# First loads of a two-layer decoder trunk: weight pieces of two contraction blocks, the first weight rounded by VectorE, and narrower zero products ahead of them

## The chip, the core and the metric

The kernel runs on one core of one Trainium2 chip. The metric is the device time of one execution in microseconds (us), as the median of several runs. A profile is taken of one execution; its span is the time from the first to the last instruction that the profile shows, and the execution's own time is a little longer than that span. Engines are named as in the profile: PE is TensorE's matmul, PEld its weight load, DVE is VectorE, ACT is ScalarE, POOL is GpSimd, and SP (SPq) is SyncE, which here only issues DMAs.

## The reference, cut to what matters

The program computes two decoder layers on 1024 tokens of 1024 features, in float32. The first has a causal Conformer convolution, the second has windowed attention; each is followed by a layer norm, an MLP with a squared ReLU, a second norm, and a gated embedding. Only the beginning bears on this change:

```python
def conformer_conv(x, w_in, b_in, w_dw, b_dw, ln_g, ln_b, w_out, b_out):
    h = x @ w_in + b_in                       # (1024 x 1024) @ (1024 x 2048)
    a, gate = jnp.split(h, 2, axis=-1)
    h = a * jax.nn.sigmoid(gate)
    ...                                       # depthwise conv, norm, silu, w_out

def reference(x, p, ...):
    for i in range(DEPTH):
        y = conformer_conv(x, ...) if i < N_A_LAYERS else swa_sink_attention(...)
        x = layer_norm(DEEPNORM_ALPHA * x + y, mix_ln_g[i], mix_ln_b[i])
        x = layer_norm(DEEPNORM_ALPHA * x + sq_relu_mlp(x, ...), mlp_ln_g[i], mlp_ln_b[i])
        x = x + (p[i] @ ple_w_proj[i]) * jax.nn.sigmoid(x @ ple_w_gate[i])
    return x
```

## The kernel before, in words

**Products in three parts.** Every large product is made of float32 values split in two: a rounded high part (`xh`, `wh`: a cast to the type fp32r) and a low part, the difference of value and high part (`xl`, `wl`). `split` does this with an ACT cast and a DVE subtraction. `mm3` then issues three matmuls for each product: high by high, high by low, low by high.

**The start.** `conv` calls `warm_up` (line 918), which clears a tile `t` of 128x512 on DVE and issues `WARM` = 8 matmuls of it on PE. Their result is used by nothing. Then the first chunk of the input product is loaded. The contraction over 1024 features is cut into eight blocks kb = 0 to 7. For each block come a slice of the transposed input, 128x512 (256 KB, into a tile `X`: 512 of the 1024 tokens), and a piece of the first weights, 128x256 (128 KB, a quarter of a tile `raw` of 128x1024; `raw` of blocks 0 to 3 and `raw` of blocks 4 to 7). `prep` with `blocks` (line 552) does this: for each block it issues two DMAs, the weight piece first except in block 0, and splits the weight piece (ACT cast to `wh`, DVE subtraction to `wl`) and the input slice (ACT cast to `xh`, DVE subtraction to `xl`). `conv_in` then issues, block by block, two products (gate and value, into two PSUM tiles), hence six matmuls of 128x512 for each block, 48 in all. After them the second 512 tokens follow with the same weights.

**What sets the order.** The program is first recorded as a list of operations, and `Recorder.schedule` then places all of them, of the whole program, in one order for each engine: it keeps a time for every engine, gives each operation an estimated duration (`cost`) and takes the operation of least number among those that are ready. A few operations may go to either DVE or POOL. Tiles come from numbered slots, which are handed on when the last user of the earlier tile is placed as done. So a change in the first operations shifts the planner's times for everything later, and with them the order in which operations that are ready at about the same time are placed. The planner counts a 512-column matmul as 227 ns, one of 128 columns as 109 ns, and a DMA's landing by its size and by how many came before it. On the chip the engines run these orders as they are, each in its own queue, and wait on semaphores.

**The rest.** After the first chunk come seven more chunks of input weights, five of them through forms that save one product in eight; the depthwise convolution as small matmuls `ps<-B,E` of 128x256, fed by an exchange through DRAM (`scr`); norms; the MLP, with intermediate values in DRAM (`hid`); attention; the second MLP; and the output.

Of the kernel before, what the change touches and what calls it, by code (L numbers as in the profile page):

```python
# [10 lines left out]
F32 = mybir.dt.float32  # L11
F32R = mybir.dt.float32r
AF = mybir.ActivationFunctionType
ALU = mybir.AluOpType

P = 128
# [4 lines left out]
HT = 512  # L21
# [32 lines left out]
             ps=6, tr=2, sc=0, pv=0, mid=0)  # L54
# [7 lines left out]
FORM_HOMES = ("A", 9), ("bo", 2), ("v", 1), ("B", 4), ("X", 8)  # L62
LATE = 50
SOONER = 200
WARM = 8
LOW_BY = 500
EMBED_BY = (300, 0)
MARK = (1, 2)
# [457 lines left out]
class Emit:  # L526
# [36 lines left out]
    def prep(self, ap, blocks=None, low=None, halves=False):  # L563

        nc = self.nc
        if halves:
            wh = nc.tile("wh", (P, 1024), F32R)
            wl = nc.tile("wl", (P, 1024), F32R)
            for w, src in ((wh, ap), (wl, low)):
                nc.sync.dma_start(w.bitcast(F32)[:, 0 : low.n], src)  # L570
            return wh, wl
        raw = nc.tile("raw", (P, 1024), F32)
        wh = nc.tile("wh", (P, 1024), F32R)
        wl = nc.tile("wl", (P, 1024), F32R)
        if blocks:
            for j, kb in enumerate(blocks):
                cs = slice(j * 256, (j + 1) * 256)
                x = self.sb("X")
                for w, k in ((x, 0), (raw[:, cs], 1))[:: -1 if kb else 1]:
                    nc.sync.dma_start(w, ap[:, cs] if k else self.d["xT"][kb, :, 0:HT])  # L580
                self.split(raw[:, cs], wh[:, cs], wl[:, cs])
                self.split(x, *self.xs(kb, 0, HT))
            return wh, wl
        if low is not None:
            c = slice(0, low.n)
            nc.sync.dma_start(raw[:, c], ap)
            nc.scalar.copy(wh[:, c], raw[:, c])
            nc.sync.dma_start(wl.bitcast(F32)[:, c], low)
            return wh, wl
        nc.sync.dma_start(raw, ap)  # L590
        nc.scalar.copy(wh, raw)
        nc.vector.tensor_tensor(out=wl, in0=raw, in1=wh.bitcast(F32), op=ALU.subtract)
        return wh, wl
# [324 lines left out]
    def warm_up(self):  # L918

        nc = self.nc  # L920
        z = self.sb("t", F32R)
        nc.vector.memset(z.bitcast(F32), 0.0)
        ps = self.ps()
        for k in range(WARM):
            nc.tensor.matmul(ps, z[:, 0:P], z, start=True, stop=True)

    def load_xT(self, h, kb):
        raw = self.sb("X")
# [1448 lines left out]
```

## Time and profile before

| | us |
|---|---|
| median of 3 runs | 2090.38 |
| lowest and highest of them | 2089.67 and 2091.93 |
| the profiled execution's own time | 2089.28 |
| its span in the profile | 2087.6 |
| PE busy in the span | 2077.5 |
| DVE busy | 1688.1 |
| ACT busy | 1228.2 |
| POOL busy | 275.2 |

The profile's page gives the busy time of each engine and a chain of waits that ended last. The timeline lists instructions by start and duration, with the idle time before them and what ended it in square brackets, where it was idle. The view by windows gives the busy time of each engine in stretches of the span, with the number of instructions, the granted clock of TensorE (PEclk), the share of the DMA engines' time that was busy, and the rate moved. A matmul's modelled duration overlaps the next one's, so its pace is read from start to start.

### The profile page before, as it was taken

Reading aid. Unit: us, or ns where it says so; the run is one execution under the profiler, and the core shown is the slowest. Engines: PE = TensorE matmul, PEld = TensorE weight load, DVE = VectorE, ACT = ScalarE, POOL = GpSimd, SP = SyncE. Lnnn points to the kernel's source line nnn. Section 1 sums busy time; section 2 is a strip of 40 time slices with the busy share of each in tenths; the row PEclk is TensorE's granted clock in tenths of the full one; section 3 lists DMA queues with packets and bytes.
Section 4 is the critical chain, followed back from the end, with each engine's and each line's share of the span. In section 5 each row is a group of like instructions: output and inputs, shape, how many; then the busy total and the mean of one; then the engine's idle time right before and its main releaser. Section 6 shows DMA issues by size and latency. Waiting matters only on the chain.

```text
span 2087.6 us, 29481 instructions
## 1 busy us (share of the span) xinstructions
PE 2077.5 (100%) x9784; PEld 1731.2 (83%) x9784; DVE 1688.1 (81%) x2628; ACT 1228.2 (59%) x2268; POOL 275.2 (13%) x512
## 2 busy tenths in 40 slices
PE   9999999999999999999999999999999999999999
PEld 7888888888888888888888888888888888888877
DVE  8999796878876789986983677869788778888688
ACT  6767656856655644454752678866666573333374
POOL 0524111000000000001220366500000000000041
PEclk9999999999999999999999999999999999999999
DMA  6669855988995879876468685698888886575636
GB/s 227 189 205 298 284 196 176 339 288 285 306 307 193 309 274 312 276 265 242 165 220 295 227 289 196 191 338 303 270 296 296 290 298 202 183 246 173 236 112 206
DMA packets 249864, 521.96 MB, mean 250 GB/s; under 512 B 25456, under 2 KB 64112, under 8 KB 249712
## 3 DMA queue, kind: packets, MB, share of 16 engines
q1 hardware_dynamic: 249712, 520.09, 73.8%
q8 instruction: 77, 1.26, 0.2%
q14 instruction: 75, 0.61, 0.1%
HBM read 348.81 MB, written 168.56 MB: 248 GB/s over the span
## 4 chain that ended last, share of the span: by engine, by line
PE 91%; DVE 4%; ACT 2%; DMA 2%; issue 1%; POOL 1%; SPq 0%; DVEq 0%; ACTq 0%; POOLq 0%
PE ps L493 74%; PE tr L493 18%; DVE g L493 1%; ACT z L493 1%; DVE sm L493 1%; POOL sm L493 1%; DVE E L493 0%; DMA raw<-in_w_in_dram 0%; DVE z L493 0%; DMA z<-in_w_dw_dram 0%; DVE t L493 0%; DMA A<-mid 0%; DVE wl L493 0%; DMA raw<-in_w_up_dram 0%; DVE B L493 0%
## 5 line engine op out<-in xcount | busy, mean ns | idle before, releaser
L493 PE MATMUL ps<-xh,xl 128*128 128x512 f32 x618 | 240.4, 389 | 0.0
L493 PE MATMUL ps<-xl,xh 128*128 128x512 f32 x618 | 240.4, 389 | 0.0
L493 PE MATMUL ps<-xh 128*128 128x512 f32 x618 | 240.4, 389 | 0.0
L493 PE MATMUL ps<-xh,wh 128*128 128x512 f32 x588 | 230.5, 393 | 0.4 <-DVE g L493 0.4
L493 PE MATMUL ps<-xl,wh 128*128 128x512 f32 x588 | 230.3, 392 | 0.2 <-DVE xl L493 0.2
L493 PE MATMUL ps<-xh,wl 128*128 128x512 f32 x588 | 230.3, 392 | 0.0
L493 POOL TENSOR_SCALAR sm<-sm 128x1 f32<-128x1 f32 x72 | 26.5, 370 | 1397.4 <-DVE E L493 1209.0
L493 PE MATMUL ps<-wh,xh 128*128 128x512 f32 x436 | 172.3, 397 | 1.6 <-DVE t L493 0.9
L493 PE MATMUL ps<-wl,xh 128*128 128x512 f32 x436 | 172.4, 396 | 0.0
L493 PE MATMUL ps<-wh,xl 128*128 128x512 f32 x436 | 172.2, 396 | 0.0
L493 ACT CAST wh<-raw 128x1024 fp32r<-128x1024 f32 (+2 forms) x134 | 119.6, 894 | 80.7 <-PE ps L493 49.9
L493 DVE TENSOR_TENSOR wl<-raw,wh 128x1024 fp32r<-128x1024 f32 (+2 forms) x100 | 99.3, 995 | 50.7 <-ACT wh L493 50.0
L493 ACT CAST wh<-g 128x512 fp32r<-128x512 f32 x136 | 81.1, 619 | 96.5 <-PE ps L493 40.5
L493 ACT CAST xh<-wh 128x1024 fp32r<-128x1024 f32 x76 | 79.8, 1050 | 96.1 <-PE ps L493 74.9
L493 PEld LDWEIGHTS ps<-xh 128*128 128x128 f32 x618 | 116.0, 188 | 24.2
L493 PEld LDWEIGHTS ps<-xh,xl 128*128 128x128 f32 x618 | 116.0, 188 | 24.1
L493 PEld LDWEIGHTS ps<-xl,xh 128*128 128x128 f32 x618 | 116.0, 188 | 23.9
L493 PEld LDWEIGHTS ps<-xh,wh 128*128 128x128 f32 x588 | 110.8, 188 | 23.1 <-DVE g L493 0.8
L493 PEld LDWEIGHTS ps<-xh,wl 128*128 128x128 f32 x588 | 110.6, 188 | 22.8
L493 PEld LDWEIGHTS ps<-xl,wh 128*128 128x128 f32 x588 | 110.8, 188 | 22.6 <-DVE xl L493 0.5
L493 DVE TENSOR_TENSOR xl<-wh,xh 128x1024 fp32r<-128x1024 f32 x76 | 92.7, 1220 | 25.3 <-ACT xh L493 25.3
L493 ACT ACTIVATE t<-t 128x512 f32<-128x512 f32 x144 | 90.8, 632 | 36.1 <-DVE t L493 34.5
(407 smaller groups left out, 5430.6 us busy)
## 6 DMA issues: line engine op xcount, KB each, us to landing
wh<-hid SPq DMA_DIRECT2D x78, 512.0 KB, 4.7
raw<-in_w_up_dram SPq DMA_DIRECT2D x68, 512.0 KB, 4.3
wl<-in_w_down_dram SPq DMA_DIRECT2D x58, 512.0 KB, 5.4
hid<-zz SPq DMA_DIRECT2D x96, 256.0 KB, 4.8
hid<-t SPq DMA_DIRECT2D x64, 256.0 KB, 5.1
z<-in_w_dw_dram SPq DMA_DIRECT2D x56, 288.0 KB, 4.1
raw<-hid SPq DMA_DIRECT2D x30, 512.0 KB, 4.7
A<-mid SPq DMA_DIRECT2D x48, 256.0 KB, 4.8
```

The source lines that it names most:

```text
L493: getattr(getattr(nc, o.eng), o.name)(*a, **k)
```

## The change

There are four edits, all at the start of the program:

- `WARM` is 14 in place of 8, and the cleared tile is the first 128 columns of `t`, so that each of the zero products has 128 columns in place of 512.
- Weight pieces are loaded by a table `PIECES`: blocks 0 and 1 have a piece of their own (128x256), blocks 2, 4 and 6 fetch a piece for two blocks (128x512, 256 KB), and blocks 3, 5 and 7 fetch none. ACT's cast and DVE's subtraction work on the same pieces.
- The rounding of block 0's weight piece is a DVE copy in place of an ACT cast.
- The order in the record is: in block 0 the input slice and then the weight piece; in all others the weight piece, its split, and then the input slice.

```diff
-WARM = 8
+WARM = 14
+PIECES = 1, 1, 2, 0, 2, 0, 2, 0
...
             for j, kb in enumerate(blocks):
-                cs = slice(j * 256, (j + 1) * 256)
+                n = PIECES[kb]
+                cs = slice(j * 256, (j + n) * 256)
                 x = self.sb("X")
-                for w, k in ((x, 0), (raw[:, cs], 1))[:: -1 if kb else 1]:
-                    nc.sync.dma_start(w, ap[:, cs] if k else self.d["xT"][kb, :, 0:HT])
-                self.split(raw[:, cs], wh[:, cs], wl[:, cs])
+                src = self.d["xT"][kb, :, 0:HT]
+                if kb == 0:
+                    nc.sync.dma_start(x, src)
+                if n:
+                    nc.sync.dma_start(raw[:, cs], ap[:, cs])
+                    (nc.scalar.copy if kb else nc.vector.tensor_copy)(wh[:, cs], raw[:, cs])
+                    nc.vector.tensor_tensor(out=wl[:, cs], in0=raw[:, cs], in1=wh[:, cs].bitcast(F32), op=ALU.subtract)
+                if kb:
+                    nc.sync.dma_start(x, src)
                 self.split(x, *self.xs(kb, 0, HT))
...
-        z = self.sb("t", F32R)
+        z = self.sb("t", F32R)[:, 0:P]
         nc.vector.memset(z.bitcast(F32), 0.0)
         ps = self.ps()
         for k in range(WARM):
-            nc.tensor.matmul(ps, z[:, 0:P], z, start=True, stop=True)
+            nc.tensor.matmul(ps[:, 0:P], z, z, start=True, stop=True)
```

What this makes of the queues is seen in three places. Line 493 before and line 494 after are the same line of the recorder, through which every operation is issued. First the DMA queue of SP, from the program's first DMA on: `X_31` to `X_36` are the input slices of blocks 0 to 5, `raw_1` holds the weights of blocks 0 to 3 and `raw_2` those of blocks 4 to 7. Before:

```order
L493 DMA X_31_95<-in_xT_dram 128x512
L493 DMA raw_1_65<-in_w_in_dram 128x256 x2
L493 DMA X_32_96<-in_xT_dram 128x512
L493 DMA raw_1_65<-in_w_in_dram 128x256
L493 DMA X_33_97<-in_xT_dram 128x512
L493 DMA raw_1_65<-in_w_in_dram 128x256
L493 DMA X_34_98<-in_xT_dram 128x512
L493 DMA raw_2_66<-in_w_in_dram 128x256
L493 DMA X_35_99<-in_xT_dram 128x512
```

And of the change:

```order
L494 DMA X_31_95<-in_xT_dram 128x512
L494 DMA raw_1_65<-in_w_in_dram 128x256 x2
L494 DMA X_32_96<-in_xT_dram 128x512
L494 DMA raw_1_65<-in_w_in_dram 128x512
L494 DMA X_33_97<-in_xT_dram 128x512
L494 DMA X_34_98<-in_xT_dram 128x512
L494 DMA raw_2_66<-in_w_in_dram 128x512
L494 DMA X_35_99<-in_xT_dram 128x512
```

The slice of block 2 (`X_33`) is the sixth DMA in both, but block 3's weights now travel ahead of it; the slice of block 3 (`X_34`) has the same bytes ahead of it in one DMA fewer.

Second the queue of DVE, from its first instruction (the clearing of the tile for the zero products) on, with `xl_242` and `wl_8` as the low parts of blocks 0 to 3. Before:

```order
L493 MEMSET t_53_117 128x512
L493 TENSOR_TENSOR xl_242_306<-X_31_95,xh_241_305 128x512
L493 TENSOR_TENSOR wl_8_72<-raw_1_65,wh_3_67 128x256 x2
L493 TENSOR_TENSOR xl_242_306<-X_32_96,xh_241_305 128x512
L493 TENSOR_TENSOR wl_8_72<-raw_1_65,wh_3_67 128x256
L493 TENSOR_TENSOR xl_242_306<-X_33_97,xh_241_305 128x512
L493 TENSOR_TENSOR wl_8_72<-raw_1_65,wh_3_67 128x256
```

And of the change:

```order
L494 MEMSET t_53_117 128x128
L494 CAST wh_3_67<-raw_1_65 128x256
L494 TENSOR_TENSOR xl_242_306<-X_31_95,xh_241_305 128x512
L494 TENSOR_TENSOR wl_8_72<-raw_1_65,wh_3_67 128x256 x2
L494 TENSOR_TENSOR xl_242_306<-X_32_96,xh_241_305 128x512
L494 TENSOR_TENSOR wl_8_72<-raw_1_65,wh_3_67 128x512
L494 TENSOR_TENSOR xl_242_306<-X_33_97,xh_241_305 128x512
```

The cast of block 0's weights stands ahead of block 0's first subtraction, and the subtraction for blocks 2 and 3 is one instruction, ahead of block 2's `xl`.

Third the queue of PE some 300 rows into the program, in the depthwise convolution (`ps<-B,E`) among a later chunk's products (`ps_400`), with a group of four transposes (`tr_81`). Before:

```order
L493 MATMUL ps_400_879<-xh_245_309,wh_388_823 128x512
L493 MATMUL ps_400_879<-xl_246_310,wh_388_823 128x512
L493 MATMUL ps_400_879<-xh_245_309,wl_389_826 128x512
L493 MATMUL ps_418_1016<-B_413_979,E_41_105 128x256 x2
L493 MATMUL tr_81_145<-ident_303,g_402_911 128x2x4x16 x4
L493 MATMUL ps_418_1016<-B_413_979,E_41_105 128x256 x7
```

And of the change:

```order
L494 MATMUL tr_81_145<-ident_303,g_399_882 128x2x4x16 x4
L494 MATMUL ps_400_887<-xh_245_309,wl_390_824 128x512
L494 MATMUL ps_400_887<-xh_245_309,wh_389_821 128x512
L494 MATMUL ps_400_887<-xl_246_310,wh_389_821 128x512
L494 MATMUL ps_400_887<-xh_245_309,wl_390_824 128x512
L494 MATMUL ps_418_1014<-B_412_976,E_41_105 128x256 x9
```

No edit touches this part of the program: the planner placed the transposes some six matmuls sooner. Such shifts stand in all queues, in the convolution and the first norms above all, and again in attention and near the end. The number of instructions on each engine changes only by the edits: PE issues 6 matmuls more, DVE 2 instructions fewer, ACT 4 fewer, SP 3 fewer, POOL the same.

## The prediction

> **What bounds the kernel now.** I read the page first, then what PE waited for (us in total, times, longest), then two stretches of the view by windows (engine busy times, then PEclk, DMA share, GB/s).
>
> ```profile
> span 2087.6 us, 29481 instructions
> ...
> PE 2077.5 (100%) x9784; PEld 1731.2 (83%) x9784; DVE 1688.1 (81%) x2628; ACT 1228.2 (59%) x2268; POOL 275.2 (13%) x512
> ```
>
> ```profile
> PE ps L493 <- DVE t L493: 2.4, 2, 1.5
> PE tr L493 <- ACT t L493: 1.1, 1, 1.1
> PE ps L493 <- DVE z L493: 0.5, 3, 0.2
> PE ps L493 <- DVE xh L493: 0.5, 1, 0.5
> PE ps L493 <- DVE g L493: 0.4, 1, 0.4
> PE ps L493 <- ACT t L493: 0.3, 1, 0.3
> PE ps L493 <- DVE xl L493: 0.2, 1, 0.2
> ```
>
> ```profile
> 20.00:50.00 30.00, 30.00 (x134) 24.82 (x134) 29.29 (x48) 19.51 (x33) 0.00 (x0) 1.00 0.56 204
> 2000.00:2088.00 88.00, 82.37 (x395) 67.79 (x393) 72.95 (x119) 48.49 (x88) 19.26 (x23) 0.99 0.56 188
> ```
>
> PE is idle for 10.1 us of the span (2087.6 - 2077.5). Most of it is the program's two ends: 1.5 us ahead of the first matmul, and part of the 5.6 in the last stretch (88.00 - 82.37). Its waits on other engines are 5.4 us in all; without the first 1.5 and the 0.2 for `xl`, which are at the start, 3.7 are left for all the rest of the program. So PE bounds nearly everything, and an edit counts by the PE time that it frees or spoils. The profiled execution took 2089.28, 1.10 below the median of 2090.38; that much is added to every sum below. A measurement of this kernel can tell about 0.2% from no change: 4.2 us, so faster means below 2086.2 and slower above 2094.6.
>
> The start is the exception, since there PE runs on what has landed. The timeline of PE, then that of ACT, then the chain of waits:
>
> ```profile
> 1.51 3.78 PE L493 MATMUL ps<-t 128*128 128x512 f32 x8 [1.51 <-DVE t L493]
> 5.09 1.05 PE L493 MATMUL ps<-xh,wh 128*128 128x512 f32 x2
> 5.94 1.03 PE L493 MATMUL ps<-xl,wh 128*128 128x512 f32 x2
> 6.79 0.65 PE L493 MATMUL ps<-xh,wl 128*128 128x512 f32 x2
> ...
> 9.46 0.50 PE L493 MATMUL ps<-xl,wh 128*128 128x512 f32 x1 [0.22 <-DVE xl L493]
> ```
>
> ```profile
> 3.57 0.62 ACT L493 CAST xh<-X 128x512 fp32r<-128x512 f32 x1 [1.50 <-DMA X<-in_xT_dram]
> 4.10 0.40 ACT L493 CAST wh<-raw 128x256 fp32r<-128x256 f32 x1
> ```
>
> ```profile
> 3.12 4.92 DMA X<-in_xT_dram
> ...
> 8.06 0.63 ACT xh L493
> ...
> 9.46 70.00 PE ps L493 x325
> ```
>
> Two things are to be seen. **First**, block 0's operands were ready at 4.50 (4.10 + 0.40), but its first matmul started at 5.09, right behind the eight zero products. **Second**, the chain does not go through that. The start ends at 9.46, when block 2's `xl` exists: its slice was issued at 3.12 and landed at 8.04, and after ACT's cast, which ends at 8.69, DVE's subtraction takes the rest. From 9.46 PE runs 70 us without a gap.
>
> **The change, part by part.**
>
> *Zero products.* Matmuls of 512 columns start 0.427 us apart up to 6.79 (0.85 for each pair: 5.09, 5.94, 6.79) and later
>
> ```profile
> 12.13 0.39 PE L493 MATMUL ps<-xh,wh 128*128 128x512 f32 x1
> 12.36 0.39 PE L493 MATMUL ps<-xl,wh 128*128 128x512 f32 x1
> 79.46 0.44 PE tr L493 x4
> ```
>
> 0.227 apart: half pace until about 7.0. (PEclk is 1.00 in the window 6 to 7 below as well, so here it is the spacing that shows the pace.) The clearing,
>
> ```profile
> 0.97 0.48 DVE L493 MEMSET t<- 128x512 f32 x1 [0.97 <-PEq L2369]
> ```
>
> gets a quarter of the columns: between 0.12 and 0.48 us; PE then starts between 1.15 and 1.51. No row has a 128-column product at half pace. Below, a quarter of 0.427 is 0.107 each, 1.5 us for 14; above, the transposes of 128 columns take 0.11 each at full pace, times 0.427/0.227 is 0.21, 2.9 us. The zeros end between 2.7 and 4.4. I take 4.2, since the transpose row is a matmul of this width.
>
> *First weight on DVE.* DVE has been idle since 1.45. No row shows this copy; the nearest is
>
> ```profile
> 262.59 0.41 DVE L493 CAST xh<-t 128x512 fp32r<-128x512 f32 x1
> ```
>
> twice its columns, so it takes 0.2 to 0.41. ACT's cast of the same piece showed no wait at 4.10, so the piece was there by then: `wh` is ready between 3.8 and 4.5, and `xh` at 4.19. If the copy ends after 4.19 it holds back block 0's `xl` behind it on DVE, by 0.3 at most; that is wanted only two matmuls (0.85) later. So block 0 starts at about 4.3 rather than 5.09, a gain of 0.8 there (0.55 to 0.85).
>
> *Two-block pieces.* They remove three DMAs, three ACT casts and three DVE subtractions of 128x256. None of those was on the chain: ACT took block 2's slice at 8.06, 0.02 after it landed. What counts is the DMA order. Ahead of block 2's slice there were 128 KB of weights for blocks 0, 1 and 2 each; now block 3's go ahead too. The rate in the neighbourhood:
>
> ```profile
> 6.00:7.00 1.00, 1.00 (x4) 0.80 (x3) 0.69 (x1) 0.45 (x2) 0.00 (x0) 1.00 0.62 162
> 8.00:9.00 1.00, 1.00 (x5) 0.53 (x3) 0.29 (x1) 0.93 (x2) 0.00 (x0) 1.00 1.04 382
> 9.00:10.00 1.00, 0.78 (x3) 0.48 (x3) 0.99 (x3) 0.90 (x2) 0.00 (x0) 1.00 1.07 397
> ```
>
> 131 KB at 382 to 397 GB/s are 0.34 us, at 162 they are 0.81. From below: the transfer was not steady. In the window 6 to 7 the DMA engines were busy for only 0.62 of the time, with many loads issued. The loads of `raw` in the first 20 us, from issue to landing:
>
> ```profile
> DMA to landing us min/median/max: 2.6/4.8/6.4
> ```
>
> Against their least, 2.6 us, the 4.92 of block 2's slice is slow, so it could land up to 2.3 sooner even with more bytes ahead (-2.0 net). I take +0.34: between 8 and 10 the engines were full, and 8.04 stands at that edge.
>
> *The sum at the start.* Block 0 at half pace from 4.3: six matmuls, to 6.86. Block 1's `xl`, and below it that of block 4, in DVE's timeline:
>
> ```profile
> 6.23 0.69 DVE L493 TENSOR_TENSOR xl<-X,xh 128x512 fp32r<-128x512 f32 x1 [0.65 <-ACT xh L493]
> ...
> 10.81 0.69 DVE L493 TENSOR_TENSOR xl<-X,xh 128x512 fp32r<-128x512 f32 x1
> ```
>
> The first was ready at 6.92, in time for block 1's third matmul, so block 1 runs from 6.86 at 0.227 each to 8.2. Then PE has used up its lead: block 2's slice lands at 8.04 + 0.34 = 8.38, and with cast, subtraction and start as long as before (9.46 - 8.04 = 1.42) PE starts its `xl` at 9.80. All of the 0.8 gained before is spent waiting, and the start ends **0.34 us later** than 9.46. What is late next is block 4: its `xl` was done at 11.50 (10.81 + 0.69) and is first wanted 12 matmuls after 9.46, at 12.2; 0.34 later for both leaves the cover of 0.7 whole. Block 3's slice has the same bytes ahead as before.
>
> *The rest of the program.* No instruction is added there, and the counts on each engine differ by the edits alone, but the planner's order is shifted in many places (the third place shown with the change). I put that at nothing. A better order could free at most the 3.7 us that PE waits there, and not likely more than 3; upward there is no such bound, and I take as much again, +3.
>
> Sum: 2089.28 + 0.34 + 1.10 = **2090.7**.
>
> **A rule against the change.** The half pace ended near 7.0, after 5.5 us in which PE always had work. The Trainium skill, "TensorE: Matmul & The Clock Gate", section "What's actually happening", says that a free-running window of about 3.4 us must be busy before the clock doubles, and that an idle one halves it. The trace agrees in that the doubling comes once, within two such windows of the first matmul. By that rule a pause between shorter zeros and the first real product can cost a window; by the trace row at 79.46 there is hardly a pause. With the pause, the sum would be that of the second rival.
>
> **The rivals.**
>
> 1. *Block 2's slice lands sooner* (the idle DMA engines at 6 to 7 us were that execution's accident, or larger pieces avoid it). Then PE goes from block 1 straight on: block 2's first matmul at 8.2, its `xl` product near 8.5 rather than 9.46, -1.0: 2089.4. For it: share 0.62. Against: the DMA rows before and after are full.
>
> 2. *Half pace lasts longer.* If the zeros end at 2.7, PE pauses 1.6 us. If the 5.5 us are counted anew from 4.3, half pace lasts until 9.8: 13 matmuls by then, where before the fifteenth had started; two at 0.227 are +0.5. If it lasts through block 3, 24 matmuls take 10.25 us, to 14.55, where before they were done at 12.0: +2.6, 2093.0. Still within 0.2%.
>
> 3. *The shifted order opens waits: slower.* In 20 to 50 us DVE was busy for 29.29 of 30, and PE had no idle only because DVE was in time. Later it was not:
>
> ```profile
> 179.34 0.50 PE L493 MATMUL ps<-xh,wh 128*128 128x512 f32 x1 [0.43 <-DVE g L493]
> ```
>
> Here, at the end of the convolution, whatever the order adds to DVE's work ahead of `g` PE waits one for one. It decides the result from 3.9 us on (4.2 - 0.34), nearly four times the longest wait of 1.1: 2094.6 and up, say 2095.5. Against: the shift shown moves transposes past some six matmuls, about 1.2 us of PE, and PE's waits say that such distances are mostly covered.
>
> 4. *The shifted order closes waits*: 3 of the 3.7 us, with rival 1: 2089.28 - 1.0 - 3.0 + 1.10 = 2086.4, at the bound of faster.
>
> That the edits do not do as they say would need block 0 to start at 5.09 again; that is 2090.7 as well, since the start ends with block 2.
>
> **How the numbers follow.** The forecast gets 0.5; rival 1 gets 0.2, rival 2 gets 0.1, rival 3 gets 0.12, rival 4 gets 0.08. Predicted is the likeliest case, 2090.7. The range takes in rivals 1 and 2 and the order's +/-3 around the forecast: 2087.7 to 2093.7. Outside remain most of rivals 3 and 4, somewhat under 0.2. Faster by over 0.2% is most of rival 4, 0.06; slower is most of rival 3, 0.1; within 0.2% the other 0.84.
>
> **What would show it.** Right: first real matmul near 4.3; PE then waiting for block 2, its `xl` product at 9.8; matmuls 0.227 apart from about 7.0; PE's busy time plus idle elsewhere as before within 3 us. Wrong: zeros that end by 3 and half pace beyond 8; block 2's `xl` product ahead of 9.2; new PE waits of 1 us between 100 and 400 or 1000 and 1400 us. The forecast itself falls if the end of the start and the total move by different amounts of more than 3 us: then the order, not the loads, made the time.

## The result, and the profile after

| | us |
|---|---|
| changed kernel, median of 21 runs | 2094.41 (2092.15 to 2097.26) |
| kernel before, median of 21 runs beside it | 2090.82 (2089.64 to 2093.51) |
| ratio, 95% interval | 1.0015 [1.0009, 1.0021] |
| profiled execution of the changed kernel | 2093.16, span 2091.4 |

The change makes the kernel 3.6 us slower: within the 0.2% that the prediction called no change, and 0.7 us above the upper end of its range. The page of the changed kernel (busy time of each engine, number of instructions), and then what PE waited for:

```profile
span 2091.4 us, 29472 instructions
...
PE 2078.4 (99%) x9790; PEld 1732.2 (83%) x9790; DVE 1687.8 (81%) x2626; ACT 1229.0 (59%) x2264; POOL 278.3 (13%) x512
```

```profile
PE ps L494 <- DVE t L494: 2.0, 2, 1.1
PE tr L494 <- ACT t L494: 1.1, 1, 1.1
PE ps L494 <- DVE g L494: 0.9, 1, 0.9
PE ps L494 <- DMA wh<-gate_t: 0.8, 1, 0.8
PE tr L494 <- DVE g L494: 0.8, 1, 0.8
PE ps L494 <- DVE E L494: 0.7, 1, 0.7
```

PE's busy time grew by 0.9, its idle time from 10.1 to 13.0 us (2091.4 - 2078.4). The waits for `g` (twice), for `E` and for a load of `wh` (at 1029 us, which e12 below has too, in the order of before) are new or longer. The start, in PE's timeline and in the chain of waits:

```profile
1.11 3.25 PE L494 MATMUL ps<-t 128*128 128x128 f32 x14 [1.11 <-DVE t L494]
4.49 1.19 PE L494 MATMUL ps<-xh,wh 128*128 128x512 f32 x2
...
8.14 0.39 PE L494 MATMUL ps<-xl,wh 128*128 128x512 f32 x1
...
9.46 0.51 PE L494 MATMUL ps<-xh,wh 128*128 128x512 f32 x1 [0.23 <-ACT xh L494]
10.18 0.50 PE L494 MATMUL ps<-xl,wh 128*128 128x512 f32 x1 [0.22 <-DVE xl L494]
```

```profile
3.11 5.65 DMA X<-in_xT_dram
8.78 0.63 ACT xh L494
9.44 0.70 DVE xl L494
10.18 3.94 PE ps L494 x16
```

Block 0 starts at 4.49 in place of 5.09. As forecast, that gain is spent waiting for block 2's slice, which lands at 8.76; the start ends at 10.18 rather than 9.46, 0.7 later. That explains a fifth of the loss. Where the rest is, the view by windows tells (columns as in the prediction). Before:

```profile
100.00:120.00 20.00, 20.00 (x117) 17.57 (x116) 19.44 (x31) 12.83 (x26) 3.71 (x7) 1.00 0.68 205
120.00:240.00 120.00, 119.45 (x693) 104.34 (x692) 102.30 (x151) 83.89 (x164) 33.50 (x52) 1.00 0.85 265
300.00:1000.00 700.00, 700.00 (x3133) 579.57 (x3131) 569.53 (x844) 398.14 (x631) 20.84 (x39) 1.00 0.79 272
```

And of the changed kernel:

```profile
100.00:120.00 20.00, 18.48 (x104) 15.56 (x103) 16.37 (x26) 12.52 (x24) 5.16 (x9) 1.00 0.65 187
120.00:240.00 120.00, 118.86 (x682) 103.81 (x681) 102.70 (x151) 83.96 (x164) 34.29 (x52) 1.00 0.84 259
300.00:1000.00 700.00, 700.00 (x3129) 579.71 (x3128) 568.93 (x839) 395.46 (x624) 18.02 (x33) 1.00 0.79 272
```

Between 100 and 120 us PE had no idle before; now it has 1.52 (20.00 - 18.48). Set beside each other by the columns of work done (when PE has passed the same number of matmul columns), PE's delay against before is 0.7 at the end of the start, grows by 2.0 near 109 us, by some 0.5 up to 240, and by less than 1 in the rest. The place at 109 us in the changed kernel, in the timelines of POOL, ACT, DVE and PE:

```profile
97.62 3.00 POOL L494 TENSOR_TENSOR cst<-cst,z 128x256 f32<-128x256 f32 x1
100.56 0.10 POOL L494 MEMSET B<- 128x16 f32 x1
```

```profile
100.65 0.51 ACT L494 ACTIVATE z<-B,cst 128x256 f32<-128x256 f32 x1 [1.59 <-POOL B L494]
...
103.23 1.05 ACT L494 CAST wh<-raw 128x1024 fp32r<-128x1024 f32 x1 [1.10 <-PE ps L494]
```

```profile
101.77 1.02 DVE L494 TENSOR_TENSOR t<-t,t 128x512 f32<-128x512 f32 x1 [1.75 <-ACT t L494]
104.31 1.23 DVE L494 TENSOR_TENSOR wl<-raw,wh 128x1024 fp32r<-128x1024 f32 x1 [1.52 <-ACT wh L494]
```

```profile
109.70 0.66 PE L494 MATMUL tr<-ident,g 128*128 128x128 f32 x4 [0.79 <-DVE g L494]
111.09 1.34 PE L494 MATMUL ps<-B,E 128*128 128x256 f32 x9 [0.73 <-DVE E L494]
```

The same work before, ACT's cast, DVE's subtraction and PE's transposes and products:

```profile
100.70 1.05 ACT L493 CAST wh<-raw 128x1024 fp32r<-128x1024 f32 x1 [0.49 <-DMA raw<-in_w_in_dram]
```

```profile
101.78 1.32 DVE L493 TENSOR_TENSOR wl<-raw,wh 128x1024 fp32r<-128x1024 f32 x1 [0.36 <-ACT wh L493]
...
105.66 0.69 DVE L493 TENSOR_TENSOR g<-g,ps 64x512 f32<-64x512 f32 x1
```

```profile
108.55 0.60 PE L493 MATMUL tr<-ident,g 128*128 128x128 f32 x4
...
112.21 1.23 PE L493 MATMUL ps<-B,E 128*128 128x256 f32 x9
```

Two things went wrong there. ACT stood 1.59 us until POOL, behind a product of 3.00 us, had cleared `B`, and with it DVE 1.75 us. Then ACT's cast of a 512 KB weight piece waited for its load: issued at 96.84, its 16 queues landed at 100.54 first, 101.07 in the median and 103.15 last, 6.31 us after the issue; before it was 4.21 (96.41 to 100.62). (The profile names PE's `ps` for ACT's wait; the last queue's landing at 103.15 fits the cast's start at 103.23.) So DVE idles for 3.3 us (1.75 + 1.52) where it idled for 0.36 before. Before, `g` was done at 106.35 (105.66 + 0.69), 2.2 us ahead of PE's transposes at 108.55; now PE, which also has nine small products placed ahead of large ones, has to wait. The 0.5 up to 240 us goes with the wait that the third rival named, 0.43 at 179.34 before and longer now:

```profile
182.14 0.50 PE L494 MATMUL ps<-xh,wh 128*128 128x512 f32 x1 [0.89 <-DVE g L494]
```

### The profile page after: what moved, and what is told of

Same layout as the page of the kernel before. It is cut to its first block, busy times and chain, and to the rows that moved or that the text cites. A ratio compares the mean times of both kernels' runs of the same rounds, so it can differ in the third digit from the quotient of the medians.

```text
span 2091.4 us, 29472 instructions
## 1 busy us (share of the span) xinstructions
PE 2078.4 (99%) x9790; PEld 1732.2 (83%) x9790; DVE 1687.8 (81%) x2626; ACT 1229.0 (59%) x2264; POOL 278.3 (13%) x512
## 3 DMA queue, kind: packets, MB, share of 16 engines
q8 instruction: 77, 1.26, 0.2%
## 4 chain that ended last, share of the span: by engine, by line
PE 92%; DVE 2%; ACT 2%; DMA 2%; issue 1%; POOL 1%; SPq 0%; DVEq 0%; ACTq 0%; POOLq 0%
PE ps L494 73%; PE tr L494 19%; ACT z L494 1%; POOL sm L494 1%; DVE sm L494 0%; DVE E L494 0%; DMA wh<-gate_t 0%; DMA z<-in_w_dw_dram 0%; DVE z L494 0%; DMA E<-B 0%; DMA raw<-in_w_in_dram 0%; DMA X<-in_xT_dram 0%; DVE g L494 0%; DMA scr<-zz 0%; DVE t L494 0%
## 5 line engine op out<-in xcount | busy, mean ns | idle before, releaser
L494 PE MATMUL ps<-xh 128*128 128x512 f32 x636 | 247.4, 389 | 0.0
L494 PE MATMUL ps<-xl,xh 128*128 128x512 f32 x636 | 247.4, 389 | 0.0
L494 PE MATMUL ps<-xh,xl 128*128 128x512 f32 x636 | 247.4, 389 | 0.0
L494 PE MATMUL ps<-xh,wh 128*128 128x512 f32 x564 | 221.3, 394 | 1.5 <-DVE g L494 0.9
L494 PE MATMUL ps<-xl,wh 128*128 128x512 f32 x564 | 220.8, 392 | 0.2 <-DVE xl L494 0.2
L494 PE MATMUL ps<-xh,wl 128*128 128x512 f32 x564 | 220.9, 392 | 0.0
L494 PE MATMUL ps<-wh,xh 128*128 128x512 f32 x368 | 146.0, 397 | 2.4 <-DVE t L494 0.9
L494 PE MATMUL ps<-wl,xh 128*128 128x512 f32 x368 | 145.6, 396 | 0.0
L494 PE MATMUL ps<-wh,xl 128*128 128x512 f32 x368 | 145.4, 396 | 0.0
L494 DVE TENSOR_TENSOR wl<-raw,wh 128x512 fp32r<-128x512 f32 (+2 forms) x97 | 98.4, 1015 | 54.0 <-ACT wh L494 53.2
```

The costliest lines, as they stand in the source:

```text
L494: getattr(getattr(nc, o.eng), o.name)(*a, **k)
```

## The experiments

Two suspects stand against each other: the edits at the start themselves, and the planner's order that they shift in the rest. So the experiments build kernels in which each part comes from one program or the other. `START` gives the edits that are made; the planner is run a second time for the program named by `ORDER`, and every instruction after the first chunk's loads takes the place in its engine's queue, the engine and the tile slots of that plan. Later kernels also put rows lo to hi of an engine's queue (`BACK`) into the other plan's order. The core of it; the short diffs further down are against its lines `START = AFTER` and `ORDER = BEFORE`, those with `BACK` against the kernel e6:

```diff
+BEFORE = dict(zeros=(8, 512), pieces=(1,) * 8, first="scalar")
+AFTER = dict(zeros=(14, 128), pieces=(1, 1, 2, 0, 2, 0, 2, 0), first="vector")
+START = AFTER
+ORDER = BEFORE
...
-                n = PIECES[kb]
+                n = self.begin["pieces"][kb]
...
-            for o in self.schedule():
+            for o in self.ordered(plan):
...
+        n, cols = self.begin["zeros"]
...
-        for k in range(WARM):
...
+        for k in range(n):
```

### The start against the order

The start of the change in the order of before (e1, the two lines as above), and the start of before in the order of the change (e2, the two names exchanged):

> The four edits at the start as in the change, but every later instruction stands in the order that the planner gave the kernel before. Theory A (the shifted order costs most): slower than before by 0.7 us, all of it by the end of the start, where block 2's low part reaches PE at about 10.2 rather than 9.46; no wait of 0.8 us at transposes near 109 us. Theory B (the start costs all of it: the later start, and the loads that then meet others): slower by 3 to 4 us, with the wait near 109 us as in the change.

> The start of the kernel before, but every later instruction in the order that the planner gave the changed kernel. Theory A: slower by 2.5 to 3.0 us, some 2 of it as PE's waits at transposes and small products between 105 and 115 us, where a weight load lands late. Theory B: within 0.5 us of before.

Then, in the order of before, the narrow zeros with the first weight on DVE (e3), and the two-block pieces alone (e4):

```diff
-START = AFTER
+START = {**BEFORE, "zeros": AFTER["zeros"], "first": "vector"}
```

```diff
-START = AFTER
+START = {**BEFORE, "pieces": AFTER["pieces"]}
```

> Only the 14 narrow zero products and the rounding of the first weight by VectorE; weight pieces of one block each, and the order of before for the rest. Theory A: block 0's first product near 4.5 rather than 5.09, and the end of the start at 9.46 as before, since block 2's slice has no more bytes ahead: total within 0.5 us of before. A rival, that the narrower zeros delay the end of half pace: up to 0.3 us slower if half pace ends near 8 us, since block 2's slice hides that.

> Only the weight pieces of two blocks; zero products and rounding as before, and the order of before for the rest. If block 3's weights ahead of block 2's slice are what moves the end of the start: 0.35 to 0.7 us later there, and in total. If the landing near 8.8 us was an accident of the profiled execution: the end of the start within 0.2 of 9.46, total within 0.3 us of before.

Measured against 33 runs of the kernel before (2090.91), with 11 runs of each:

| | us | ratio, interval |
|---|---|---|
| e1: change's start, order of before | 2093.36 | 1.0012 [1.0003, 1.0021] |
| e2: start of before, change's order | 2093.18 | 1.0009 [1.0000, 1.0018] |
| e3: narrow zeros, first weight on DVE | 2091.77 | 1.0003 [0.9994, 1.0012] |
| e4: two-block pieces | 2091.62 | 1.0005 [0.9996, 1.0014] |

By the medians neither suspect is alone: start and order each cost about 2.3 us without the other, though together only 3.6. The interval of e2 begins at 1.0000, so this run by itself doesn't show the order's part; e15 and e16 below do. The order without any edit shows the changed kernel's waits: 0.79 for `g`, 0.73 for `E`, PE idle for 1.51 of 100 to 120 us; but its weight load was late too (6.40). The two single edits are too small for these intervals.

In e1's profile part of the delay is the clock. PE's granted clock falls once more in mid-program, where PE is partly idle:

```profile
260.00:265.00 5.00, 3.40 (x24) 2.65 (x23) 5.00 (x13) 4.00 (x9) 4.65 (x8) 0.99 1.00 328
265.00:270.00 5.00, 5.00 (x22) 4.15 (x22) 4.77 (x10) 3.51 (x8) 3.90 (x6) 0.66 0.94 313
```

One window of 3.41 us at half pace: set beside before by the columns of work done, PE's delay grows by 1.3 us there (1.69 at 262 us, 2.98 at 270). Three more profiles show it (e2, e3, and e6 below); those of before, of the change and of e4 don't. PE is idle there for 1.8 us in the change's profile too (260 to 270 us), so what decides is where the windows fall, which differs from run to run. Each of the nineteen traces can be cut into windows of 3.41 us from the end of its half pace at the start on, up to 2080 us. Of the windows at full pace, half pace follows the seven in which PE was idle for 1.60 us or more (e1 and e3 1.60, e2 1.69, e6 1.70, e10 2.26, e8 2.48, e9 2.80), and none in which it was idle for 1.57 (e7, the most) or less. That was found afterwards and not tested.

### Once more the two programs, and two smaller edits

> The program of before once more, for a second profile of it. If what its first profile shows is typical: the end of the start within 0.2 us of 9.46, the weight load issued near 96.5 us landing after 4.2 us, no PE wait between 100 and 120 us, TensorE at full clock from the first window of 3.41 us that begins after the zero products. If the first profile was a lucky one: a landing after 5.7 us or more, and a PE wait of about 1 us near 114, as the runs of the two starts had it with the same order.

> The changed program once more, for a second profile of it. If the shifted order is what makes PE wait: again 0.8 and 0.7 us at transposes and small products near 110 us. If the narrow zero products do not count as work for the clock: half pace until the second end of a 3.41 us window after them (8.0 to 11.3 us), not the first. Block 2's low part reaches PE between 10.0 and 10.4 us.

In one execution each, the kernel before took 2091.22 and the changed one 2095.69. The first repeats the place at 109 us without a wait, the second with waits of 0.38, 0.78 and 0.73. The end of the start is not steady: block 2's `xl` product starts at 9.16 here for before and at 11.15 for the change (the slice took 6.61 us to land, not 5.65).

Next the change with PE's rows 501 to 540 (108 to 117 us) back in the order of before (e6), and, in the order of before, six wide zeros in place of eight and the first weight on DVE (e7):

```diff
-ORDER = BEFORE
+ORDER = AFTER
+BACK = (BEFORE, ("tensor", 501, 540))
```

```diff
-START = AFTER
+START = {**BEFORE, "zeros": (6, 512), "first": "vector"}
```

> The changed kernel with 39 matmuls of PE's queue, near 109 to 117 us, put back in the order that the planner gave them before (transposes and the first depthwise product of nine stand behind 2 and 20 large matmuls again); all other queues as in the change. If PE's place for them makes the waits: the two waits of 0.8 and 0.7 us vanish or shrink to one below 0.5, and the total is 1.0 to 1.5 us below the changed kernel's, at 2.0 to 2.6 us above before. If the work ahead of them on VectorE and ScalarE is late however PE is ordered: as slow as the changed kernel within 0.5 us, with the waits a few matmuls further on.

> Six zero products of 512 columns, the first weight rounded by VectorE, weight pieces of one block each, and the order of before for all the rest. Block 0's first product near 4.3 rather than 5.09; if wide zeros count as work for the clock, half pace ends with the first 3.41 us window that begins after 1.5 us, between 4.9 and 8.3. Block 2's slice still ends the start, at 9.4 to 9.7; total within 0.7 us of before. A rival, that the early start itself costs: 1 us or more above before.

e6: 2093.68, 1.0013 [1.0004, 1.0022]. PE's waits near 109 us shrink to 0.32 and 0.34, but the start ended at 11.15 in its profile and the clock fell at 268 us; the median is 0.7 under the change's, less than the intervals can tell. e7: 2091.12, 1.0002 [0.9993, 1.0011]: block 0 starts at 4.29, block 2 at 9.64, and no time is gained. That bears out the prediction's point by itself, within this interval: an earlier block 0 is worth nothing as long as block 2's slice lands when it does.

### Rows of single engines put back

The change with SP's rows of 95 to 100 us back, with PE's rows (e8) and without (e9); and the kernel before with PE's rows in the change's order (e10):

```diff
-BACK = (BEFORE, ("tensor", 501, 540))
+BACK = (BEFORE, ("tensor", 501, 540), ("sync", 50, 57))
```

```diff
-BACK = (BEFORE, ("tensor", 501, 540))
+BACK = (BEFORE, ("sync", 50, 57))
```

```diff
-START = AFTER
-ORDER = AFTER
-BACK = (BEFORE, ("tensor", 501, 540))
+START = BEFORE
+ORDER = BEFORE
+BACK = (AFTER, ("tensor", 501, 540))
```

> The change, with PE's rows around 108 to 117 us and SP's rows around 95 to 100 us (two writes of kept, the weight load raw, two loads z and one load B) put back into the order that the program before has there. In the four profiles with the change's order so far the weight load took 6.3 to 6.9 us to land (6.31, 6.40, 6.91, 6.30); in the six with the order of before it took 4.2, 4.2, 4.5, 4.5 and twice about 6 (5.76, 6.02). Theory L (SP's order makes the weight load late): it lands 4.2 to 4.5 us after its issue, PE has no wait over 0.2 us for g or E between 105 and 117 us, and the time is about 2092.4 (1.0 for the start and some tenths from the rest). Theory C (the late landing is chance in both orders): it lands late in about half of all runs, here too, whatever stands around it in the queue.

> The change, with SP's rows around 95 to 100 us alone put back; PE keeps the change's order, with the transposes and 18 small products placed sooner. Theory L: the weight load lands after 4.2 to 4.5 us, g is some 2 us ahead of PE, no wait for g over 0.2 us near 109, and the time is about 2092.4. Theory P (PE's order alone makes the wait, by wanting E and g too soon): PE waits 0.7 to 0.8 us twice near 109 to 111 us as in the change, and the time stays at 2094.4. If both are needed: no wait over 0.2 us, 2092.4, as for L, but then the kernel with PE's order alone shows none either.

> The program before, with PE's rows around 108 to 117 us alone in the change's order. Theory P: waits of 0.7 to 0.8 us twice near 109 to 111 us though the weight load lands after 4.2 to 4.5 us, and about 2093. Theory L: no such wait where the weight load lands after 4.2 to 4.5 us, 2090.9. Theory C: where it lands after 6 us by chance, the waits are there.

All three came out slower than the change: e8 2096.68, 1.0027 [1.0018, 1.0037]; e9 2100.18, 1.0036 [1.0024, 1.0049]; e10 2096.22, 1.0023 [1.0014, 1.0032]. None of the theories foresaw that. In e8 SP's old order puts a load `z` behind `raw` and `B`, while ACT's queue, still that of the change, wants that `z` first. ACT, PE, and two stretches of the windows in e8:

```profile
104.75 0.67 ACT L568 CAST E<-z 128x576 fp32r<-128x576 f32 x1 [5.87 <-DMA z<-in_w_dw_dram]
```

```profile
111.88 1.22 PE L568 MATMUL ps<-A,wh 128*128 128x512 f32 x2 [2.81 <-ACT t L568]
```

```profile
112.00:116.00 4.00, 4.00 (x14) 3.23 (x15) 3.91 (x7) 2.81 (x6) 0.97 (x1) 0.63 0.30 81
116.00:120.00 4.00, 4.00 (x28) 3.64 (x27) 4.00 (x9) 2.19 (x4) 0.00 (x0) 1.00 0.69 186
```

ACT stands still for 5.87 us, PE for 2.81, and the pause then costs a window at half pace as well (PEclk 0.63). In e10 PE's order of the change meets DVE's order of before, and PE waits 3.29 us for `E`, with the weight load on time (4.42), then two windows at half pace. So e10 bears out theory P in that PE's shifted rows alone make a wait; but its size says that the rows of the engines belong together: three of the four kernels with rows of one or two engines moved came out slower than the change, and e6 was no faster by more than the intervals can tell. Theory L fell: in e8 and e9 the load was late again (5.95 and 5.78) with SP's rows as before.

Last, the change with the rows of all five engines up to about 118 us in the order of before (e11):

```diff
-BACK = (BEFORE, ("tensor", 501, 540))
+BACK = (BEFORE, ("tensor", 0, 540), ("sync", 0, 68), ("scalar", 0, 142), ("vector", 0, 144), ("gpsimd", 0, 50))
```

> The change, with the rows of all five engines up to about 118 us put back into the order of the program before, and the change's order from there on. The three kernels before this one moved the rows of one or two engines alone and made the place worse (delay of PE by 4.5 to 6 us at 109 to 115 us, and one or two windows at half pace after the pause). Theory W (the orders of the engines there fit only together, and the change's as a whole costs 2 us): ACT has no wait of 1.6 us for POOL ahead of its cast of the weights, DVE none of 1.75 us for ACT's t, PE waits for neither g nor E by more than 0.2 us where the weight load lands within 4.5 us, and PE's delay against before is the same at 117 us as at the end of the start; the time is about 2092.4 (2094.4 less 2.0), or about 2093.5 where the weight load lands late and PE waits 1.0 for E. Theory S (the order at this place is not what costs): the time stays at 2094.4 though the place shows no wait.

e11: 2095.42, 1.0019 [1.0010, 1.0028]: not 2092.4. ACT's wait for POOL and DVE's 1.75 us for `t` are gone, as expected, but the load was late (6.24), PE waits 1.07 for `E` at 115.77 and 1.15 more at 122.02, where the order changes back to the change's. Theory W holds for the waits. The time doesn't decide: W had 2093.5 for a late load, its rival, that the order at this place is not what costs, 2094.4, and the interval takes in both; in its profile PE was already 1.97 late at 12 us, where half pace lasted to 12.4. It left one question: why is this load late so often?

### The late load: instruction fetches

The trace records a DMA queue of instruction fetches whose 77 pieces of 16 KB make 1.26 MB in the kernel before: 64 bytes (1.26 MB / 19568) for each of PE's 9784 matmuls and as many weight loads, so they are taken for PE's; one starts with every 254 of these on average (19568 / 77). (A second such queue, 75 pieces of 8 KB, had a piece just ahead of this load's landing in e2 alone, at 100.25.) In the stretch of 99 to 101.5 us the DMA view of the changed kernel (queue, kind: packets, MB, share) shows one, starting at 100.61, while the weight load is about to land; the second profile of before has none there, its nearest starts at 104.35 (the first had one at 99.99, and its load was on time):

```profile
q1 hardware_dynamic: 254, 0.67, 80.2%
q8 instruction: 1, 0.02, 2.6%
```

```profile
q1 hardware_dynamic: 457, 0.79, 99.1%
```

Six zeros more are 12 PE instructions more ahead of everything, so a fetch after a set number of them comes sooner in the work, by some 1.1 us here (an estimate: 12 of the 254 that take some 23 us). Three kernels in the order of before test it: the kernel before with six zeros of 128 columns behind the eight wide ones and no other edit (e12); the narrow start with 54 zeros of 32 columns (e13); and the narrow start with eight zeros (e14).

```diff
-START = AFTER
+START = {**BEFORE, "more": 6}
...
+        for k in range(self.begin.get("more", 0)):
+            nc.tensor.matmul(ps[:, 0:P], z[:, 0:P], z[:, 0:P], start=True, stop=True)
```

```diff
-START = AFTER
+START = {**BEFORE, "zeros": (54, 32), "first": "vector"}
```

```diff
-START = AFTER
+START = {**BEFORE, "zeros": (8, 128), "first": "vector"}
```

> The program before, with six zero products of 128 columns behind the eight of 512 (PE as many instructions as the change, no other edit). Theory F (an instruction fetch of PE's inside the weight load makes its last queue late; PE's count of instructions sets where the fetch stands): the fetch starts near 100 us and the load lands 5.8 us or more after its issue; ACT's cast, DVE and PE's E are late and PE waits about 1.0 us near 113 us; 2092.0. Theory Z (the narrow zeros, or what they do to the clock at the start, make it late): the load lands after 4.2 to 4.5 us and PE does not wait near 113; 2091.0, as before.

> The start with narrow zeros and the first weight on DVE, in the order of before, with 54 zero products of 32 columns in place of 14 of 128: PE has 46 matmuls and 46 weight loads more than before, so the fetch (256 instructions each, about 24 us apart there) stands some 8 us sooner than in before, at 92 to 97 us. Theory F: no fetch inside the load's last 2 us, and it lands after 4.2 to 4.5 us, without a wait of PE near 113. Theory Z: it lands after 5.8 us or more, as with the 14 narrow ones, and PE waits about 1.0 us near 113. The time itself may be longer by what the 54 zeros take at the start.

> The start with eight zeros of 128 columns, the first weight on DVE, single pieces, in the order of before: as many PE instructions as before. Theory F: the fetch stands where it does in the profiles of before (at 100 to 101 us in two of four, at 104.4 us in the other two), and the load is on time, as in those four; PE does not wait near 113; 2091.0, or 0.3 to 1.4 us more if the half pace, which then lasts longer, is no more hidden at the start. Theory Z: the load lands 5.8 us or more after its issue, and PE waits about 1.0 us near 113.

| | fetch starts | load, issue to last landing | PE's wait near 113 us | us (ratio, interval) |
|---|---|---|---|---|
| e12: eight wide and six narrow zeros | 100.48 | 6.15 | 1.04 | 2092.89 (1.0009 [1.0000, 1.0018]) |
| e13: 54 zeros of 32 columns | 100.89, load issued at 105.17 | 4.27 | none | 2099.96 (1.0044 [1.0032, 1.0057]) |
| e14: eight narrow zeros | 104.31 | 4.30 | none | 2091.18 (1.0001 [0.9993, 1.0010]) |

All three go with theory F and against theory Z, though e12's interval begins at 1.0000. In e13 the zeros took 11.7 us and everything behind them came 8.6 us later, so the fetch did not come sooner, contrary to what was expected; instead the load came later, and so was clear of it all the same. In the other eighteen profiles this fetch started at 99.9 to 102.1 us in all nine with the change's 14 zeros or e12's six more; at 100.0 to 100.9 in three and 104.3 to 104.6 in three of the six with as many PE instructions as before; and at 102.9 to 104.4 in the three with fewer (e7, and e15 and e16 below). So the count shifts the odds; it doesn't set the place alone. e12 is the plainest: ACT, PE, and the DMA view of the same 2.5 us, with not one edit but six useless matmuls:

```profile
103.09 1.05 ACT L513 CAST wh<-raw 128x1024 fp32r<-128x1024 f32 x1 [2.43 <-DMA raw<-in_w_in_dram]
```

```profile
114.15 1.34 PE L513 MATMUL ps<-B,E 128*128 128x256 f32 x9 [1.04 <-DVE E L513]
```

```profile
q1 hardware_dynamic: 316, 0.64, 80.0%
q8 instruction: 1, 0.02, 2.3%
```

Over all nineteen profiles (those of before, of the change, and of the kernels above and below), a fetch started within 1.6 us ahead of the load's median landing in twelve. In ten of them the last queue landed 5.8 to 6.9 us after the issue, and in two (before, e4) on time, 4.2 and 4.5. In the seven others the load took 4.2 to 4.9 us in six and 5.6 in one. In the ten late ones a single queue is late: it landed 0.8 to 1.9 us after the fifteenth (103.15 against 101.75 in the change), in the other nine 0.3 at most. That a fetch at this place is what delays the last queue is thus well borne out; by what (a shared DMA engine, say) the trace doesn't tell, since it names no engine for a packet, and the three exceptions stay unexplained.

### What the late load and the order each cost

The pieces and the first weight of the change with 4 zeros of 128 columns in place of 14, in the change's order (e15) and in that of before (e16):

```diff
-START = AFTER
-ORDER = BEFORE
+START = {**AFTER, "zeros": (4, 128)}
+ORDER = AFTER
```

```diff
-START = AFTER
+START = {**AFTER, "zeros": (4, 128)}
```

> The change, in its own order, with 4 zero products of 128 columns in place of 14 (they end near 2 us; block 0 still starts near 4.3). Theory F (the instruction fetch makes the load late, and the late load makes the loss near 109 us): the fetch stands at 102 us or later, the load lands within 4.6 us, DVE's wait of 1.5 us for the cast wh goes and its 1.75 us for t stays, PE's waits for g and E near 109 to 111 us fall from 1.5 together to under 0.4, and the time is about 2092.5. Theory O (the change's order makes the loss, late load or not): the load on time, but PE's two waits stay at 1 us or more together, 2094.4.

> The change's pieces and first weight with 4 narrow zeros, all later instructions in the order of before. Theory F: fetch at 102 us or later, load within 4.6 us, no wait of PE over 0.2 us between 105 and 117 us; what is left is the start's 0.6 to 1.7: 2091.5 to 2092.6, and 2091.7 by the kernel with two-block pieces alone. Theory O gives the same here. If the time stays at the 2093.4 of the kernel with 14 zeros, both fall.

e16: 2091.69, 1.0007 [0.9999, 1.0016]; fetch at 104.39, load 4.88, and hardly a PE wait at the place. e15: 2095.11, 1.0024 [1.0014, 1.0035]; fetch at 102.93, load 5.56, not the 4.6 expected, DVE's wait for the cast down to 0.75, PE's wait for `g` gone, the one for `E` as before. e16's window, then e15's window and wait:

```profile
100.00:120.00 20.00, 19.93 (x114) 17.16 (x113) 18.80 (x29) 13.05 (x25) 4.08 (x7) 1.00 0.65 199
```

```profile
100.00:120.00 20.00, 19.22 (x109) 16.25 (x108) 17.12 (x27) 12.85 (x24) 5.62 (x9) 1.00 0.66 198
```

```profile
110.76 1.34 PE L513 MATMUL ps<-B,E 128*128 128x256 f32 x9 [0.73 <-DVE E L513]
```

At the place itself the load sooner by 0.75 us saves PE 0.74 (1.52 less 0.78), and 0.78 stays. For the whole program theory O is nearer: with the same start, the change's order is 3.4 us slower than that of before (2095.11 against 2091.69, measured side by side; the intervals of the two ratios don't quite part, but the lowest of e15's eight runs, 2092.68, lies above nine of e16's eleven). No kernel beat the one before.

By the columns of work done, each against the first profile of before, the two parts can be told apart at this place. This is how much PE's delay grows between 105 and 119 us:

| | load on time | load late |
|---|---|---|
| order of before | 0.0 (b_again, e4, e7, e13, e14), 0.4 (e16) | 1.3 (e1), 1.5 (e3), 1.6 (e12) |
| the change's order | no profile | 2.2 (the change, e2), 2.8 (a_again); 1.4 (e15, 5.56) |

(The kernels with moved rows are left out.) So in the order of before the late load alone makes 1.3 to 1.6 us there. What the change's order alone makes isn't shown, since no profile has it with a load under 5.5 us. Elsewhere profiles of one program differ by as much: b_again falls 2.1 us behind the first profile of before after 300 us.

## Why the prediction was wrong

The step that failed is "The rest of the program": "I put that at nothing". The shifted order costs time there: 3.4 us between two kernels with the same start (e15 against e16), and 2.3 by the medians with no edit at the start (e2, whose interval begins at 1.0000). Point by point:

- *Zeros and first weight.* The zeros start 0.21 apart (the fourteenth at 3.94, 2.83 after the first), as the row of transposes had it; the first starts at 1.11, just ahead of the forecast 1.15 to 1.51. DVE's copy took 0.29, within its 0.2 to 0.41, and ended at 4.34; block 0 starts behind it at 4.49, forecast 4.3. That the earlier block 0 is worth nothing was right, and e7 shows it.
- *Half pace, the second rival.* Its mechanism is there, nearly free of charge. With wide zeros, in all seven profiles, half pace ended with the first window of 3.41 us that began after the first zero; with narrow ones, in ten of twelve, only with the first that began after the first real product. An estimate fits all nineteen: count every matmul at the start as 0.427 us for 512 columns, so that narrow zeros 0.21 apart fill half of the time. Then half pace ended with the first window filled to 0.78 or more (e9 the least), and never with one filled to 0.77 (e2 the most) or less. It was fitted afterwards; no run tests it. In the change the half pace lasted to about 8.1 (PE's rows above) instead of 7.0, and block 2 was waited for anyway; in e11 it lasted to 12.4 and wasn't free.
- *Two-block pieces.* Right in mechanism, too small in size: the slice landed 0.72 later (8.76 against 8.04), not 0.34, and cast, subtraction and start behind it took 1.42 as forecast. It landed at 8.3 to 9.7 in the ten profiles with two-block pieces (median 8.78) and at 7.7 to 8.3 in the nine with single ones (median 8.02). The size is not steady: block 2's `xl` product started at 9.8 to 11.2 in the former, and at 9.2 to 10.0 in the latter (without e13, whose zeros last longer). By the medians the pieces alone (e4) cost 0.7 us, and with 4 narrow zeros (e16) 1.35, against 2090.34 beside it; both intervals hold no change.
- *The rest.* The third rival named the engine and the wait (DVE, `g`) and the place at 179 us, with a price from 3.9 up. There the wait grew from 0.43 to 0.89 only, and it isn't steady: 0.4 to 1.6 in the profiles with the order of before that show it, 0.6 to 1.8 in those with the change's. Most came at 109 us, 2.0. That "such distances are mostly covered" was the wrong sentence: of the 2.2 us by which `g` was ahead, the change's order spent 1.75 on ACT behind POOL, and the late load took 1.52 more. I had weighed PE's shift alone, by its six matmuls, and not that of ACT, SP and POOL ahead of DVE.
- *What was not thought of.* The six extra zeros, priced by the time they take, seem to cost a second time: they shift PE's instruction fetches, one of which then meets the weight load more often (e12: 2.0 us in the median, with an interval from 0 to 3.8; in its profile one wait of 1.04, and 0.5 at the start).
- *The range.* "I take as much again, +3" had no row behind it. In the change's profile the start's 0.7, the 2.0 near 109 us and the 0.5 up to 240 make 3.2 of the 3.8 by which its span is longer.

The fourth rival (waits that close) didn't happen. What stays open: the start's 2.4 and the order's 2.3 don't add up to 3.6, nor does the place at 109 us give all of e15's 3.4; both lie within what intervals of +/-1.9 us let stand. One part that overlaps is shown: the late load is in e1, in e2 and in the change. How much of the order's cost would stay with a load on time is open too.

## What to carry to other kernels

A change at the start of a program whose order is planned as a whole is an edit of all of it: hold the order still (or move it alone) before crediting or blaming the edit. Price a shifted order by the engine that feeds the waiting one, by its slack in that place and by what stands ahead in all of the queues; rows of one engine, judged or put back alone, misled here. An instruction added for free still shifts the fetches of those behind it, so a load with little slack may come late a hundred microseconds on, as e12's profile shows.

## What the runs showed of the hardware

- Instructions, PE's by their count, come by DMA during the run: 16 KB in 0.9 to 1.9 us, 15 to 34 us apart (before and the change). In ten of twelve profiles a 512 KB load that met such a fetch landed with its last queue 1.6 to 2.5 us behind the median one (103.15 against 101.07 in the change); in two, before and e4, it was on time.
- Zero matmuls of 128 or of 32 columns started 0.21 us apart alike (the change, e13), and 11.7 us of the latter did not end the half pace (e13, full pace from 18.0); 3.8 us of 512-column ones did (b_again, full pace from 5.5).
- A pause of PE of 2.7 to 3.3 us in mid-program was followed by one or two windows of 3.41 us at half pace (e8, e9: one; e10: two); pauses of 0.8 and 0.7 near 109 us were not. In nineteen traces, 1.60 us of PE idle in one such window was enough and 1.57 was not. The Trainium skill, "TensorE: Matmul & The Clock Gate", section "What's actually happening", has a free-running window of 3413 ns, an idle one of which brings back the half clock. The length agrees; but these pauses are shorter than a window, so a window need not be wholly idle.
